# Front of a two-layer decoder step: the first two projections on rows without 1/rms, loads alternating by channel tile, step sizes from fp32 rows

## The chip, the cores and the metric

One Trainium2 chip; the kernel runs on one of its cores. The metric is the device time of one execution in microseconds, the median of the runs. The engines are PE (matrix multiply, with PEld, its weight loads), DVE (vector), ACT (scalar functions), POOL (a second, slower vector engine) and SP (here it only issues DMAs).

## The reference, cut to what matters

Two layers, an SSD layer and a pooling layer, on 1024 prompt tokens of one sequence and 64 sample tokens (8 sequences of 8). Everything is float32. The change touches the entry into the first layer:

```
rmsnorm(x, g) = x * rsqrt(mean(x*x) + EPS) * g
mod = silu(c) @ ada_w[i] + ada_b[i]; shift, scale, gate = split(mod, 3)
hn = rmsnorm(x, norm_g[i]) * (1 + scale) + shift
zxbcdt = hn @ w_in                    # z, xbc, dt_raw
conv = conv_b + sum(xp[:, k:k + L] * conv_w[k])   # 4 taps over time, on xbc; then silu
dt = softplus(dt_raw + dt_bias)       # step sizes, one per head
```

`shift` and `scale` are vectors over the channels, one for the prompt and one for each sample sequence. Behind this come the chunked scan, a gated norm, the output projection, and the pooling layer, which the change does not touch.

## The kernel before

All activations lie transposed: 128 channels on the partitions, 1088 tokens (1024 prompt, 64 sample) along the free axis, cut into three chunks `CH` of 364, 364 and 360. The model's 1024 channels are eight such tiles, k = 0 to 7. A float32 product is made of three matmuls in the faster format fp32r: the weights are split into `hi` and `lo` (L118 on ACT, L119 on DVE), the activations too, and hi·hi, hi·lo and lo·hi are summed in PSUM (`mm1`, L159 to L163).

`setup` (L173) issues in SP's queue all eight tiles of x, then the conditioning `ct`, the vectors `vec`, the constants `kc`; PE meanwhile runs 55 idle matmuls (`warm`). `front` (L1053) then squares each x tile on ACT (L1061, L1065), adds the squares up on DVE in `rst` (L1066), sums them over partitions with a matmul by ones (`ms_log`, L275) and makes 1/rms on ACT by Ln and Exp (L278, L290). For each channel tile `ada_first` loads two halves of the block of `ada_w` (L232), multiplies them with silu(c) (L236, tile `am`), copies the result (L241, `mp`), transposes it by two small matmuls (L245) and adds biases: `shf` and `scl` (L254, L255).

The projections come in groups of six tiles of 128 output channels (two B/C tiles, two x tiles, two z tiles), eight groups. Group 0 is special. Its first two tiles (PSUM `mm` and `p`, weights `w`) run with the channel tile k as outer loop, so that each normalised tile is used as soon as `modulate` (L292 to L313) has made it: on DVE t = x·scl·rst (L297), on ACT hi = t + shf (L303), on DVE lo (L304), and five short operations for the 64 sample columns, whose scl and shf differ by sequence (L309 to L313, one of them on ACT). The same loop makes the step sizes `pdt` in plain fp32, out of hi and lo in turn, four narrow matmuls each (L1104). Tiles 3 to 6 of the group (`proj_group`, weights `wh`, `wl`) then run on the stored hi and lo.

A finished tile is moved out of PSUM by ACT (`proj_chunk`, L353, L355) and convolved over time (`conv_tile`, L316): POOL makes the first tap (L322, and L323 for the sample columns), DVE adds three taps (L325, L326), ACT takes Tanh (L330) and DVE closes the product (L331). `dt_phase` turns `pdt` into step sizes in pieces.

The order on each engine is not that of the source: a scheduler that belongs to the language sets it when the program is built. Engines run their own row strictly in that order and wait for each other by semaphores. SBUF is handed out in 31 slots of one row of tokens (`Slots`); a tile that gets a slot waits for the last reader of what lay there.

## Time and profile before

| what | us |
|---|---|
| median of 3 runs (1702.71 to 1705.88) | 1704.2 |
| the profiled execution, its own time | 1702.18 |
| its span in the trace | 1700.4 |
| busy in the span: DVE, ACT, POOL | 1232.1, 732.9, 588.6 |
| first matmul of a projection | 23.50 |
| first matmul of tile 3 of group 0 | 74.96 |
| first matmul of tile 4 of group 0 | 87.03 |
| granted TensorE clock, mean | 0.994 of full |

Busy times overlap, engines run beside each other. In rows of the timeline the columns are start, duration, engine, line, operation, output<-inputs, shape, how many rows were merged, and in brackets the idle time ahead of it and what ended it. Each fp32 matmul leaves two records, each fp32r matmul one. The duration of an instruction overlaps the next one's somewhat, so a price is better read from one start to the next.

### The profile page before, as it was taken

Reading aid. Unit: us, or ns where it says so; the run is one execution under the profiler, and the core shown is the slowest. Engines: PE = TensorE matmul, PEld = TensorE weight load, DVE = VectorE, ACT = ScalarE, POOL = GpSimd, SP = SyncE. Lnnn points to the kernel's source line nnn. Section 1 sums busy time; section 2 is a strip of 40 time slices with the busy share of each in tenths; the row PEclk is TensorE's granted clock in tenths of the full one; section 3 lists DMA queues with packets and bytes.
Section 4 is the critical chain, followed back from the end, with each engine's and each line's share of the span. In section 5 each row is a group of like instructions: output and inputs, shape, how many; then the busy total and the mean of one; then the engine's idle time right before and its main releaser. Section 6 shows DMA issues by size and latency. Waiting matters only on the chain.

```text
span 1700.4 us, 29848 instructions
## 1 busy us (share of the span) xinstructions
PE 1664.1 (98%) x11701; PEld 1581.7 (93%) x11701; DVE 1232.1 (72%) x2144; ACT 732.9 (43%) x1498; POOL 588.6 (35%) x612
## 2 busy tenths in 40 slices
PE   8999999999999999999999998999999999999997
PEld 6899999999999999997889998999999999999996
DVE  5676767687676867687788448978889996555546
ACT  5344554655555555556542027533333333221123
POOL 0224435353444435262310024455666630000012
PEclk9999999999999999999999999999999999999999
DMA  9222243324334132415874132232323368511102
GB/s 357 78 69 86 91 148 90 125 85 145 98 103 149 50 129 74 155 48 181 298 248 171 38 122 72 73 120 102 112 98 109 108 219 323 189 50 50 38 26 105
DMA packets 104460, 209.72 MB, mean 123 GB/s; under 512 B 16224, under 2 KB 56320, under 8 KB 104320
## 3 DMA queue, kind: packets, MB, share of 16 engines
q1 hardware_dynamic: 104320, 207.82, 35.6%
q8 instruction: 92, 1.51, 0.4%
q14 instruction: 48, 0.39, 0.1%
HBM read 160.95 MB, written 46.84 MB: 122 GB/s over the span
## 4 chain that ended last, share of the span: by engine, by line
PE 81%; DVE 10%; DMA 3%; ACT 2%; issue 2%; POOL 1%; SPq 0%; DVEq 0%; ACTq 0%; POOLq 0%
PE mm L161 18%; PE mm L162 18%; PE mm L163 18%; PE st L905 4%; PE st L903 4%; PE st L904 4%; PE y L547 2%; PE S L556 2%; DVE ws L769 2%; PE y L551 1%; PE am L236 1%; PE tr L497 1%; PE tr L493 1%; DVE x L693 1%; PE pdt L1104 1%
## 5 line engine op out<-in xcount | busy, mean ns | idle before, releaser
L161 PE MATMUL mm<-hh,wh 128*128 128x364 f32 (+1 forms) x1104 | 366.0, 331 | 0.0
L163 PE MATMUL mm<-hh,wl 128*128 128x364 f32 (+1 forms) x1104 | 363.0, 329 | 0.0
L162 PE MATMUL mm<-hl,wh 128*128 128x364 f32 (+1 forms) x1104 | 363.0, 329 | 0.0
L161 PE MATMUL mm<-gh,wh 128*128 128x364 f32 (+3 forms) x768 | 252.9, 330 | 4.6 <-DVE gs L696 2.6
L163 PE MATMUL mm<-gh,wl 128*128 128x364 f32 (+3 forms) x768 | 252.9, 329 | 0.0
L162 PE MATMUL mm<-gl,wh 128*128 128x364 f32 (+3 forms) x768 | 252.3, 329 | 0.2 <-DVE gl L681 0.2
L118 ACT ACTIVATE wh<-wr 128x1024 fp32r<-128x1024 f32 (+1 forms) x97 | 95.7, 986 | 283.6 <-PE mm L162 259.1
L693 DVE SCALAR_TENSOR_TENSOR x<-mm,gat,x 128x364 f32<-128x364 f32 (+3 forms) x192 | 108.9, 571 | 147.3 <-PE mm L163 146.6
L161 PEld LDWEIGHTS mm<-hh,wh 128*128 128x128 f32 x1104 | 207.6, 188 | 4.5 <-issue 2.8
L162 PEld LDWEIGHTS mm<-hl,wh 128*128 128x128 f32 x1104 | 207.5, 188 | 1.3 <-issue 1.0
L163 PEld LDWEIGHTS mm<-hh,wl 128*128 128x128 f32 x1104 | 207.5, 188 | 0.8 <-issue 0.4
L325 DVE SCALAR_TENSOR_TENSOR xbc<-raw,cwh,xbc 128x1024 f32<-128x1024 f32 x96 | 137.9, 1437 | 34.7 <-POOL xbc L322 34.7
L161 PEld LDWEIGHTS mm<-gh,wh 128*128 128x128 f32 x768 | 144.4, 188 | 7.7 <-issue 3.6
L709 POOL TENSOR_TENSOR ss<-ss,sq 128x364 f32<-128x364 f32 (+1 forms) x24 | 25.6, 1069 | 352.9 <-ACT sq L708 352.9
L162 PEld LDWEIGHTS mm<-gl,wh 128*128 128x128 f32 x768 | 144.2, 188 | 1.1 <-issue 0.6
L163 PEld LDWEIGHTS mm<-gh,wl 128*128 128x128 f32 x768 | 144.4, 188 | 0.6 <-issue 0.5
L905 PE MATMUL st<-hh,w 128*128 128x272 f32 x448 | 129.2, 288 | 0.0
L903 PE MATMUL st<-hh,w 128*128 128x272 f32 x448 | 129.2, 288 | 0.0
L904 PE MATMUL st<-hl,w 128*128 128x272 f32 x448 | 128.9, 288 | 0.0
L532 POOL TENSOR_TENSOR ea<-xbc,ea 128x512 f32<-128x512 f32 x56 | 82.8, 1479 | 119.1 <-ACT ea L491 107.7
L119 DVE TENSOR_TENSOR wl<-wr,wh 128x1024 fp32r<-128x1024 f32 (+1 forms) x97 | 109.9, 1133 | 14.2 <-ACT wh L118 14.0
L322 POOL TENSOR_SCALAR xbc<-raw,cwh 128x1024 f32<-128x1024 f32 x32 | 53.2, 1662 | 149.7 <-ACT raw L353 103.6
(279 smaller groups left out, 3966.6 us busy)
## 6 DMA issues: line engine op xcount, KB each, us to landing
wr<-win SPq DMA_DIRECT2D x48, 512.0 KB, 4.2
acb<-acd SPq DMA_DIRECT2D x64, 256.0 KB, 3.8
wr<-pin SPq DMA_DIRECT2D x32, 512.0 KB, 3.5
x<-xT SPq DMA_DIRECT2D x16, 544.0 KB, 8.1
gyd<-xbc SPq DMA_DIRECT2D x16, 544.0 KB, 2.9
gr<-gyd SPq DMA_DIRECT2D x16, 544.0 KB, 6.9
pld<-pl SPq DMA_DIRECT2D x16, 544.0 KB, 2.8
zgd<-pz SPq DMA_DIRECT2D x16, 544.0 KB, 2.7
```

Of the source, the lines that this page charges most:

```text
L118: self.nc.scalar.activation(hi[:, :nk, :], raw[:, :nk, :], AF.Copy)
L119: self.nc.vector.tensor_tensor(out=lo[:, :nk, :], in0=raw[:, :nk, :], in1=hi[:, :nk, :].bitcast(F32), op=ALU.subtract)
L161: nc.tensor.matmul(ps[:, :n], hi[:, k, :], ah[:, a:a + n], start=first, stop=False)
L162: nc.tensor.matmul(ps[:, :n], hi[:, k, :], al[:, a:a + n], start=False, stop=False)
L163: nc.tensor.matmul(ps[:, :n], lo[:, k, :], ah[:, a:a + n], start=False, stop=last)
L322: nc.gpsimd.tensor_scalar(dst[:, :NP], raw[:, 0:NP], w[0], b, op0=ALU.mult, op1=ALU.add)
L325: nc.vector.scalar_tensor_tensor(out=dst[:, :NP], in0=raw[:, k:k + NP], scalar=w[k], in1=dst[:, :NP], op0=ALU.mult, op1=ALU.add)
L532: nc.gpsimd.tensor_tensor(out=ea, in0=C[:, tok].unsqueeze(1).to_broadcast([P, 4, 128]), in1=ea, op=ALU.mult)
L693: nc.vector.scalar_tensor_tensor(out=x[d][:, a:a + pn], in0=ps[:, :pn], scalar=self.gat[l][:, d, 8:9], in1=x[d][:, a:a + pn], op0=ALU.mult ...
L903: nc.tensor.matmul(ps[c][:, :QUART], hi[:, k], xh[:, t], start=(k == 0), stop=False)
L904: nc.tensor.matmul(ps[c][:, :QUART], hi[:, k], xl[:, t], start=False, stop=False)
L905: nc.tensor.matmul(ps[c][:, :QUART], lo[:, k], xh[:, t], start=False, stop=(k == 3))
```

## The change

- Only ct is loaded ahead of x; then x and the two ada halves of channel tile 0, vec, kc, the two weight tiles, and from there on x and the ada halves of one channel tile after another (`x_load`, `ada_load`). `warm` runs 30 matmuls instead of 55.
- `raw_split` makes u = x·scl without 1/rms, split into `uh` (ACT) and `ul` (DVE), and puts ten more columns behind the 64 sample ones: shf of the nine sequences and a zero. The first two projections run on u, so that their third chunk is 370 wide and also yields the projected shift. The last four slots are ten columns longer for that.
- 1/rms is needed when these two tiles leave PSUM: `raw_chunk` multiplies by `rst` on DVE and adds the projected shift on ACT (before: one ACT copy).
- The normalised rows (`modulate`) are now made after that, beside the third projection, which has the channel tile as outer loop; the fourth to sixth run as before.
- The step sizes come from the fp32 product x·scl·rst that `modulate` leaves in x (four narrow matmuls per channel tile instead of eight); the shift comes by 32 tiny matmuls `pds` and enters as a bias in `dt_phase`.
- A staging tile `st` in the scan of the samples shares the buffer of `xl`.

```
+    def raw_split(self, k):
+        nc, x, sc = self.nc, self.xs[k], self.scl[0]
+        hi, lo = self.slots.get("uh", F32R, full=True), self.slots.get("ul", F32R, full=True)
+        nc.scalar.activation(hi[:, :NP], x[:, :NP], AF.Copy, scale=sc[:, k, 8:9])
+        nc.vector.scalar_tensor_tensor(out=lo[:, :NP], in0=x[:, :NP], scalar=sc[:, k, 8:9], in1=hi[:, :NP].bitcast(F32), op0=ALU.mult, op1=ALU.subtract)
+        t = self.mt.tile([P, 416], F32, tag="mt", bufs=2, name=self.name("us"))
...
+        nc.scalar.activation(t[:, NS:NS + 9], self.shf[0][:, k, :], AF.Copy)
+        nc.gpsimd.memset(t[:, NS + 9:NS + 10], 0.0)
+        nc.scalar.activation(hi[:, NP:SLOT], t[:, :NS + 10], AF.Copy)
+        nc.vector.tensor_tensor(out=lo[:, NP:SLOT], in0=t[:, :NS + 10], in1=hi[:, NP:SLOT].bitcast(F32), op=ALU.subtract)
+        return hi, lo
+
+    def raw_chunk(self, G, ii, c, ps, rst, sh):
...
+        nc.vector.tensor_tensor(out=o, in0=ps[:, :pn], in1=rst[:, a:a + pn], op=ALU.mult)
+        nc.scalar.activation(o, o, AF.Identity, bias=sh[:, 8:9])
...
+            self.conv_tile(G["ti"][ii], raw, dst, G["ncv"][:, ii])
...
         for k in range(8):
+            if k < 7:
+                self.x_load()
+                self.adaw.append(self.ada_load(k + 1))
+                self.ada_first(k + 1)
+            u = self.raw_split(k)
+            for i in range(2):
+                for c, (a, n) in enumerate(CH):
+                    self.mm1(pst[i][c], ws[i], k, u, (a, n + (10 if c == 2 else 0)), k == 0, k == 7)
...
+        for i in range(2):
             self.proj_begin(G, i)
+            sh = self.gp.tile([P, 9], F32, tag=f"psh{i}", name=f"psh{i}")
+            nc.scalar.activation(sh, pst[i][2][:, 360:369], AF.Copy)
+            for c in range(3):
+                self.raw_chunk(G, i, c, pst[i][c], rst, sh)
...
         for k in range(8):
             hi, lo = sl.get("hh", F32R), sl.get("hl", F32R)
-            for a, n in CH if k == 0 else ((0, TOK),):
-                self.modulate(0, k, xs[k], rst, hi, lo, a, n, xs[k][:, a:a + n])
+            self.modulate(0, k, xs[k], rst, hi, lo, 0, TOK, xs[k])
+            self.hn.append((hi, lo))
+            for c in range(3):
+                self.mm1(ps[c], w, k, (hi, lo), CH[c], k == 0, k == 7)
+            for j in range(4):
+                o, n, tp = slice(32 * j, 32 * j + 32), 320 if j == 3 else 256, (0, 32 * j)
+                nc.tensor.matmul(pdt[o, :n], wdt[:, k, :], xs[k][:, 256 * j:256 * j + n], start=k == 0, stop=k == 7, tile_position=tp)
+                nc.tensor.matmul(pds[o, :9], wdt[:, k, :], self.shf[0][:, k, :], start=k == 0, stop=k == 7, tile_position=tp)
...
-            st = gp.tile([P, 256], F32R, tag="st", bufs=1, name=self.name("st"))
+            st = gp.tile([P, 256], F32R, tag="xl", bufs=1, name=self.name("st"))
```

What the scheduler makes of it, at three places. First PE, in the loop over the channel tiles (`am` is the ada block, `uh`/`ul` and `hh`/`hl` the activations, `w` the two weight tiles with their splits). Before, from the ada block of one tile into the next:

```order
L236 MATMUL am_528<-ada_524,scp 32x256 x4
L236 MATMUL am_528<-ada_526,scp 32x256 x4
L161 MATMUL mm_346<-hh_543,w_13_308 128x364
L162 MATMUL mm_346<-hl_544,w_13_308 128x364
L163 MATMUL mm_346<-hh_543,w_14_309 128x364
L245 MATMUL am_528<-kc,mp_537 128x9 x2
L161 MATMUL mm_347<-hh_543,w_13_308 128x364
```

Now:

```order
L241 MATMUL am_459<-ada_455,scp 32x256 x4
L164 MATMUL mm_241<-uh_474,w_4_212 128x364
L164 MATMUL mm_242<-uh_474,w_4_212 128x364
L164 MATMUL mm_243<-uh_474,w_4_212 128x370
L164 MATMUL p_244<-uh_474,w_6_218 128x364
L164 MATMUL p_245<-uh_474,w_6_218 128x364
L164 MATMUL p_246<-uh_474,w_6_218 128x370
L241 MATMUL am_459<-ada_456,scp 32x256 x4
L165 MATMUL mm_241<-ul_475,w_4_212 128x364
L166 MATMUL mm_241<-uh_474,w_5_213 128x364
L165 MATMUL mm_242<-ul_475,w_4_212 128x364
L250 MATMUL am_459<-kc,mp_468 128x9 x2
```

The two ada halves now stand apart, six matmuls on `uh` between them, and the pdt matmuls are gone from the loop.

Second DVE, where the normalised rows are made (`hl` is their lo part, `xbc_781`/`xbc_798` before and `xbc_673`/`xbc_700` now are the convolved tiles 1 and 2). Before, the end of the loop over the channel tiles and the first convolution:

```order
L297 SCALAR_TENSOR_TENSOR x_154<-x_154,scl_237,rst_247 128x1024
L310 TENSOR_TENSOR x_154<-x_154,scl_237 128x64
L434 MEMSET dtu_1046 128x128
L311 TENSOR_TENSOR x_154<-x_154,shf_235 128x64
L304 SCALAR_TENSOR_TENSOR hl_738<-x_154,shf_235,hh_737 128x1024
L313 TENSOR_TENSOR hl_738<-x_154,hh_737 128x64
L325 SCALAR_TENSOR_TENSOR xbc_781<-raw_340,cwh,xbc_781 128x1024
```

Now, the end of the second convolution and the first channel tile:

```order
L330 SCALAR_TENSOR_TENSOR xbc_700<-raw_686,cwh,xbc_700 128x1024
L331 SCALAR_TENSOR_TENSOR xbc_700<-raw_686,cwh,xbc_700 128x64
L330 SCALAR_TENSOR_TENSOR xbc_700<-raw_686,cwh,xbc_700 128x1024
L336 SCALAR_TENSOR_TENSOR xbc_673<-raw_659,xbc_673 128x1088
L331 SCALAR_TENSOR_TENSOR xbc_700<-raw_686,cwh,xbc_700 128x64
L330 SCALAR_TENSOR_TENSOR xbc_700<-raw_686,cwh,xbc_700 128x1024
L331 SCALAR_TENSOR_TENSOR xbc_700<-raw_686,cwh,xbc_700 128x64
L309 SCALAR_TENSOR_TENSOR hl_736<-x_142,shf_200,hh_735 128x1024
L314 TENSOR_TENSOR x_142<-x_142,rst_222 128x64
L336 SCALAR_TENSOR_TENSOR xbc_700<-raw_686,xbc_700 128x1088
L315 TENSOR_TENSOR x_142<-x_142,scl_202 128x64
L302 SCALAR_TENSOR_TENSOR x_247<-x_247,scl_202,rst_222 128x1024
```

Before, all eight `hl` stood ahead of the convolutions; now both convolutions stand ahead of the first `hl`, and seven more channel tiles follow them.

Third ACT at the same place (`hh` is the hi part; the Tanh has the convolved tile as its input). Before:

```order
L303 ACTIVATE hh_701<-x_152,shf_235 128x1024
L312 ACTIVATE hh_701<-x_152 128x64
L241 ACTIVATE mp_653<-am_644 128x256
L303 ACTIVATE hh_737<-x_154,shf_235 128x1024
L312 ACTIVATE hh_737<-x_154 128x64
L353 ACTIVATE raw_340<-mm_346 128x364
```

Now:

```order
L308 ACTIVATE hh_735<-x_142,shf_200 128x1024
L335 ACT_TABLE_LOAD
L335 ACTIVATE raw_659<-xbc_673 128x1088
L335 ACTIVATE raw_686<-xbc_700 128x1088
L308 ACTIVATE hh_762<-x_247,shf_200 128x1024
L317 ACTIVATE hh_735<-x_142 128x64
```

The Tanh of both convolved tiles now stand between `hh` of channel tile 0 and that of channel tile 1; before, they came behind all eight.

More of the change, by code (lines that the diff above doesn't have):

```diff
@@ L57, in add_wide, with get @@
         self.pools.update({t: (pool, WIDE) for t in self.b})
-    def get(self, name, dtype=F32, wide=False, short=False):
+    def get(self, name, dtype=F32, wide=False, short=False, full=False):
         older = short and self.a and self.b and self.freed.get(self.b[0], 0) <= self.freed.get(self.a[0], 0)
-        tag = (self.b if self.b and (wide or older or not self.a) else self.a).pop(0)
+        free = self.b if self.b and (wide or older or not self.a) else self.a
+        tag = free.pop(free.index(next(t for t in free if t in self.long)) if full else 0)
         pool, w = self.pools[tag]
@@ L214, in setup, with x_load, ada_load @@
             nc.gpsimd.memset(t, 0.0)
+    def x_load(self):
+        self.xs.append(self.slots.get("x"))
+        self.nc.sync.dma_start(self.xs[-1], self.io["xT"][len(self.xs) - 1])
+    def ada_load(self, kt):
+        raws = [self.slots.get("ada") for _ in range(2)]
+        for hh in range(2):
+            self.nc.sync.dma_start(raws[hh][:, :1024].rearrange("p (a b) -> p a b", a=4), self.io["adaA"][0, kt][:, 4 * hh:4 * hh + 4, :])
+        return raws
     def warm(self, n):
@@ L1114, in front @@
+        sl.free(rst, wdts)
+        dt = self.dt_phase(pdt, pds)
+        next(dt)
+        for c in range(3):
+            self.proj_chunk(G, 2, c, ps[c])
+        for i, _ in enumerate(self.proj_group(G, 3)):
+            if i > 2:
                 next(dt, None)
```

115 lines of the change are left out of this document (53 added, 62 removed).

## The prediction

> **What bounds the kernel now.** I read the page first, then the table by stretches of time, then the timeline of the first 130 us engine by engine.
>
> ```profile
> PE 1664.1 (98%) x11701; PEld 1581.7 (93%) x11701; DVE 1232.1 (72%) x2144; ACT 732.9 (43%) x1498; POOL 588.6 (35%) x612
> ```
>
> TensorE is the bound, so a change in the front is worth whatever it moves the point from which TensorE never waits again. The stretches show where that point is now (columns: stretch, its length, busy PE, PEld, DVE, ACT, POOL with counts, granted clock, DMA share, GB/s):
>
> ```profile
> 23.50:30.10 6.60, 6.25 (x27) 3.50 (x27) 4.58 (x9) 2.10 (x4) 1.95 (x2) 0.52 1.02 407
> ...
> 50.00:60.00 10.00, 10.00 (x91) 8.22 (x93) 8.49 (x20) 5.19 (x9) 0.00 (x0) 1.00 0.19 59
> ...
> 80.00:90.00 10.00, 10.00 (x62) 10.00 (x61) 9.16 (x13) 5.88 (x9) 4.09 (x9) 1.00 0.03 7
> 90.00:100.00 10.00, 10.00 (x62) 10.00 (x61) 9.79 (x17) 2.91 (x4) 2.99 (x5) 1.00 0.14 52
> ```
>
> From 40 us on PE is busy without a gap, but between 80 and 100 us DVE is at 92 and 98%: an engine with no room left. The marks against which I hold everything are starts on PE: the first projection matmul, the first of the third projection (weights `wh`), the first of the fourth.
>
> ```profile
> 23.50 1.18 PE L161 MATMUL mm<-hh,w 128*128 128x364 f32 x2 [1.85 <-ACT hh L303]
> ...
> 74.96 0.43 PE L161 MATMUL mm<-hh,wh 128*128 128x364 f32 x1
> ...
> 87.03 0.33 PE L161 MATMUL mm<-hh,wh 128*128 128x364 f32 x1
> ```
>
> So projections 1 and 2 take 23.50 to 74.96, the third 12.07 us. All later rows of normalised x lie ready by then, so the fourth projection's start is the mark: **before, 87.03 us.** Nothing later waits (10.00 of 10.00 in every stretch), so what that mark moves, the end moves.
>
> **Part 1: the earlier start.** Loads are paced by DMA:
>
> ```profile
> 5.92 1.11 ACT L1065 ACTIVATE sq<-x 128x1088 f32<-128x1088 f32 x1 [0.25 <-DMA x<-xT]
> 7.29 1.11 ACT L1065 ACTIVATE sq<-x 128x1088 f32<-128x1088 f32 x1 [0.26 <-DMA x<-xT]
> ...
> 14.16 1.30 ACT L1065 ACTIVATE sq<-x 128x364 f32<-128x364 f32 x3 [0.29 <-DMA x<-xT]
> 18.62 0.16 PEld L236 LDWEIGHTS am<-ada,scp 128*32 128x32 f32 x8 [0.75 <-DMA ada<-adaA]
> 19.90 0.16 PEld L236 LDWEIGHTS am<-ada,scp 128*32 128x32 f32 x8 [1.12 <-DMA ada<-adaA]
> 21.16 1.06 ACT L118 ACTIVATE w<-wr 128x1024 fp32r<-128x1024 f32 x1 [0.17 <-DMA wr<-win]
> ```
>
> An x tile lands every 1.37 us, a half of an ada block or a weight tile every 1.27, and ct, vec, kc and wdt together about 3.2 (14.16 to 18.62 less one ada half). The new queue before the first product holds ct, one x (first landing 4.6 before), two ada halves, vec, kc, one weight tile. With the small ones at 2.8: 4.6 + 0.8 + 2.5 + 2.0 + 1.3 = 11.2; then ACT splits the weights (1.06) and makes uh (1.15): first matmul at **13.5 us**, 10 us earlier (12.5 to 14.5). The second channel tile needs a second weight tile, scv, x and two ada halves more (11.2 + 1.3 + 0.4 + 1.4 + 2.5 = 16.8), then the last ada half's matmuls 0.6, mp 0.4, the p2 pair and scl 1.2, a short copy 0.2, uh 1.15 and the hand-overs, 4.2 in all (prices below): PE starts k=1 at **21.0**. The weights of projection 3 now stand behind the last ada half in SP's queue and land at 16.8 + 6 x 3.9 + 1.7 = 42, long before they are needed.
>
> **Part 2: the pace of the eight channel tiles.** What PE pays per tile, from the steady loop of before:
>
> ```profile
> 37.94 0.33 PE L163 MATMUL mm<-hh,w 128*128 128x364 f32 x1
> 38.20 0.64 PE L236 MATMUL am<-ada,scp 128*32 128x256 f32 x8
> 38.77 0.43 PE L162 MATMUL mm<-hl,w 128*128 128x360 f32 x1
> ...
> 39.70 0.33 PE L163 MATMUL p<-hh,w 128*128 128x364 f32 x1
> 39.87 0.33 PE L162 MATMUL p<-hl,w 128*128 128x360 f32 x1
> ...
> 50.05 0.33 PE L163 MATMUL mm<-hh,w 128*128 128x364 f32 x1
> 50.22 0.61 PE L245 MATMUL am<-kc,mp 128*128 128x9 f32 x4
> 50.69 0.41 PE L161 MATMUL mm<-hh,w 128*128 128x364 f32 x1
> ...
> 64.72 0.32 PE L163 MATMUL p<-hh,w 128*128 128x360 f32 x1
> 64.97 0.75 PE L1104 MATMUL pdt<-hh,wdt 128*32 128x256 f32 x8
> ...
> 66.18 0.44 PE L161 MATMUL mm<-hh,w 128*128 128x364 f32 x1
> ```
>
> Start to start, a matmul is 0.167; an ada half put between two costs 38.77 - 37.94 - 0.17 = 0.66, the p2 pair 0.47, the eight pdt matmuls of hi and lo 1.29. New, per tile: 18 matmuls 3.0 (ten more columns in every third are 10/364 of 0.167: nothing), two ada halves 1.32, p2 0.47, no pdt: 4.79. One wait is added. ACT squares x of the next tile but one (1.11) ahead of uh, so from the p2 pair:
>
> ```profile
> 49.78 0.38 ACT L241 ACTIVATE mp<-am 128x256 f32<-128x256 f32 x1 [0.73 <-PE am L236]
> ...
> 50.94 0.23 DVE L254 TENSOR_SCALAR shf<-am,vec 128x9 f32<-128x9 f32 x1 [0.55 <-PE am L245]
> 51.09 0.28 DVE L255 TENSOR_SCALAR scl<-am,adab,vec 128x9 f32<-128x9 f32 x1
> ...
> 53.02 1.14 ACT L303 ACTIVATE hh<-x,shf 128x1024 fp32r<-128x1024 f32 x1
> ```
>
> shf starts 0.72 after p2, a short copy 0.2, square 1.1, uh 1.15, hand-overs: 3.35; PE has p2, ten matmuls and one ada half in that time, 2.8. It waits 0.55: **5.35 per tile**. DMA needs 1.37 + 2.54 = 3.9, DVE 1.2 + 1.2 + four short ones, ACT some 3.1: all below. The stretch 23.50:30.10 shows a clock of 0.52 behind the wait for x; such a stretch costs half of 6.6 us, and I take 2 for it behind the gap at 18 to 21. k=2 starts at 21.0 + 4.8 + 0.2 + 2 = 28.0, k=7 at 28.0 + 5 x 5.35 = 54.8.
>
> ```profile
> 16.05 2.40 PE L275 MATMUL ms<-rst,ones 128*128 128x364 f32 x6 [0.16 <-DVE rst L1066]
> ...
> 17.88 0.56 ACT L278 ACTIVATE rst<-ms,eps 128x364 f32<-128x364 f32 x1 [0.25 <-PE ms L275]
> ...
> 19.72 0.50 ACT L290 ACTIVATE rst<-rst 128x360 f32<-128x360 f32 x1
> ```
>
> Its 18 matmuls and three sums (0.8 each) end at 60.1; Ln and Exp make the last third of 1/rms ready at **61.3** (55 to 64).
>
> **Part 3: what is late next.** DVE now has everything that needs 1/rms in one row, and the third projection eats its output as it is made. Prices:
>
> ```profile
> 57.22 1.28 DVE L297 SCALAR_TENSOR_TENSOR x<-x,scl,rst 128x1024 f32<-128x1024 f32 x1
> 58.42 0.22 DVE L310 TENSOR_TENSOR x<-x,scl 128x64 f32<-128x64 f32 x1
> 58.67 0.23 DVE L311 TENSOR_TENSOR x<-x,shf 128x64 f32<-128x64 f32 x1
> 58.81 1.22 DVE L119 TENSOR_TENSOR wl<-wr,wh 128x1024 fp32r<-128x1024 f32 x1
> ...
> 74.19 1.28 DVE L325 SCALAR_TENSOR_TENSOR xbc<-raw,cwh,xbc 128x1024 f32<-128x1024 f32 x1 [7.23 <-POOL xbc L322]
> ...
> 84.89 0.48 DVE L403 SCALAR_TENSOR_TENSOR dta<-dtv 128x320 f32<-128x320 f32 x1
> ```
>
> A wide operation moves DVE on by 1.20, a short one by 0.13 to 0.25 (0.18 taken); the two convolutions with one closing product ran 74.19 to 84.89, 10.7. In the built program the wide eviction products of tiles 1 and 2 come first, then x of channel 0, then **both convolutions, then hl of channel 0**, which the third matmul of the third projection needs. Also ACT's hh of channel 1 stands behind the two Tanh, which wait for the convolutions. From 61.3: the last four evictions 1.3; x of channel 0 1.2 (63.8); POOL's first product, which the convolution waits for, by
>
> ```profile
> 72.96 1.20 POOL L322 TENSOR_SCALAR xbc<-raw,cwh 128x1024 f32<-128x1024 f32 x1 [45.71 <-ACT raw L355]
> 74.14 1.44 POOL L323 TENSOR_SCALAR xbc<-raw,cwh 128x64 f32<-128x64 f32 x1
> ```
>
> is 2.6 to 3 behind the last eviction: 65.1. Convolutions and one short operation 10.9: 76.0. Then hl of channel 0, the second closing product and 14 wide operations of channels 1 to 7: 16 x 1.20 = 19.2, and 34 short ones 6.1: the last hl at **101.3**. PE has its last nine matmuls behind it: 1.5. Fourth projection at **102.8**, 15.8 us after 87.03. PE itself needs only 12.0 for the third projection and 8 x 0.65 for pdt from the fp32 rows (half the 1.29); the 32 tiny pds matmuls fall into its wait.
>
> Behind the mark DVE has 10.9 less to do than before, since the two convolutions lie ahead of it, so I expect no new wait there. Costed at nothing, with their cover: the shared buffer of `st` and `xl` (covered by the projection matmuls woven into the scans; two short ACT copies, 0.5 us, in each of 8 groups if not); 30 for 55 warm matmuls (they run before the first load has landed); the new dt path (DVE's short operations, counted among the 34).
>
> **The sum.** The profiled run took 1702.18 (span 1700.4), 2 us under the median of the three runs, 1704.2. 1702.18 + 15.8 = 1718.0; on the median **1720**. Bounds: 1/rms at 55 or 64 (-6, +3), short operations at 0.13 or 0.25 (-2, +2), convolutions uncontended at 9.5 or 12 (-1, +1): 1711 to 1726, and 1727 with the clock below.
>
> **Clock.** PE will wait about 11 us for hl of channel 0, and the row 23.50:30.10 says what follows a wait here: half clock for 6.6 us. Nine matmuls and pdt at 0.52 are 4.1 per channel against DVE's 2 x 1.20 + 4 x 0.18 = 3.1, so one such stretch adds about 1 us, which is in the upper bound. The Trainium skill, TensorE: Matmul & The Clock Gate, Part 1, says that an idle window of about 3.4 us halves TensorE's clock and about as long a busy one restores it. By that rule the cost would be half of 3.4 us per gap, 1.7 us, less than the 2 I take behind the gap at 18 to 21; the trace's 6.6 us decides.
>
> **Rivals.**
> 1. *DVE does not gate* (faster). With 1/rms at 61.3, PE could be through the third projection at 61.3 + 2.5 + 12.0 + 5.2 = 81.0, 6 us before 87.03: 1698. It decides at DVE needing less than 24 us from 1/rms to the last hl (87.0 - 61.3 - 1.5); I count 40. For it: the earlier start is real. Against: 24 wide operations alone are 28.8, and the order is fixed when the program is built. 0.08.
> 2. *Clock stays half through the third projection* (slower still). PE's 4.1 instead of DVE's 3.1 a channel tile over 8 tiles: +8, 1728. For it: the wait is longer than any in the front now. Against: before, it came back while PE was kept busy. 0.17.
> 3. *The tiles run at the pace of the loads*, 3.9 instead of 5.35, no clock loss: 1/rms 13 us earlier, 48, and the mark at 89.5: +2.5, 1706.7, no change to be told. It decides at PE needing under 3.9; it needs 4.79. 0.05.
> 4. The forecast: 0.70.
>
> **Chances.** A measurement tells 0.2% (3.4 us) from no change. Faster 0.08 (rival 1), same 0.05 (rival 3), slower 0.87 (forecast and rival 2). The range 1711 to 1730 takes in the forecast's bounds and rival 2, and leaves out 1 and 3, 0.13.
>
> **What would show it.** First projection matmul on PE near 13.5; its starts per channel tile 5.35 apart with short waits for uh; 1/rms near 61; PE's longest wait, some 10 us, ended by DVE's first hl; DVE without gap from there to about 101; fourth projection near 103, and all behind it shifted by that much. Wrong if PE's third projection takes about 15 us instead of 40, or if the stretch behind the front shows PE idle that before did not have.

## The result and the profile after

The changed kernel takes 1727.9 us (median of four, 1725.15 to 1729.01) against 1703.5 (four runs; the 1704.2 above was of three): ratio 1.0139, 95% interval 1.0123 to 1.0154. Forecast were 1720 and a range of 1711 to 1730. The profiled execution took 1725.15 us, its span 1723.4, against 1702.18 and 1700.4; the accounts below are made with these, 23.0 us apart.

TensorE's timeline of the changed kernel first (start, duration, instruction, idle time before it and who ended it): the first products of the first three channel tiles, the longest wait, and the mark of the prediction, the fourth projection's first product.

```profile
13.33 0.60 PE L164 MATMUL mm<-uh,w 128*128 128x364 f32 x2 [1.78 <-ACT uh L1064]
22.97 0.77 PE L164 MATMUL mm<-uh,w 128*128 128x364 f32 x3 [1.77 <-ACT uh L1064]
31.45 0.77 PE L164 MATMUL mm<-uh,w 128*128 128x364 f32 x3 [1.16 <-ACT uh L1064]
37.08 0.77 PE L164 MATMUL mm<-uh,w 128*128 128x364 f32 x3 [0.49 <-ACT uh L1064]
81.69 0.67 PE L165 MATMUL mm<-hl,wh 128*128 128x364 f32 x1 [9.96 <-DVE hl L309]
107.05 0.43 PE L164 MATMUL mm<-hh,wh 128*128 128x364 f32 x1 [0.26 <-ACT raw L358]
```

The first product comes 10.2 us earlier than before, as meant. The mark comes 20.0 us later: 107.05 against 87.03. In between, ScalarE's last third of 1/rms and VectorE's row behind it (first x, first convolution product, first and last wide low part):

```profile
64.74 0.49 ACT L295 ACTIVATE rst<-rst 128x360 f32<-128x360 f32 x1
```

```profile
66.42 1.28 DVE L302 SCALAR_TENSOR_TENSOR x<-x,scl,rst 128x1024 f32<-128x1024 f32 x1
69.32 1.28 DVE L330 SCALAR_TENSOR_TENSOR xbc<-raw,cwh,xbc 128x1024 f32<-128x1024 f32 x1 [1.62 <-POOL xbc L327]
80.35 1.28 DVE L309 SCALAR_TENSOR_TENSOR hl<-x,shf,hh 128x1024 fp32r<-128x1024 f32 x1
103.02 1.28 DVE L309 SCALAR_TENSOR_TENSOR hl<-x,shf,hh 128x1024 fp32r<-128x1024 f32 x1 [0.39 <-ACT hh L308]
```

1/rms is there at 65.23, the mark 41.8 us behind it, and VectorE works nearly all that time. The table by stretches (length, busy PE, PEld, DVE, ACT, POOL, granted clock, DMA share, GB/s) shows who had work:

```profile
10.00:20.00 10.00, 7.38 (x47) 5.27 (x38) 5.46 (x8) 4.79 (x7) 0.10 (x1) 0.83 1.03 409
20.00:30.00 10.00, 7.73 (x54) 5.25 (x50) 3.93 (x9) 4.13 (x8) 0.10 (x1) 0.83 1.02 408
...
70.00:80.00 10.00, 1.74 (x68) 1.25 (x64) 9.70 (x13) 2.40 (x2) 3.50 (x6) 0.50 0.00 0
80.00:90.00 10.00, 7.07 (x26) 4.91 (x26) 10.00 (x19) 3.85 (x6) 1.63 (x4) 0.53 0.03 7
90.00:100.00 10.00, 10.00 (x64) 6.21 (x63) 10.00 (x22) 5.39 (x8) 0.00 (x0) 1.00 0.00 0
```

TensorE is busy for 1.74 of 10 us at 70 to 80 while VectorE is at 9.70 to 10.00: there the front's bound is VectorE. From 84.5 on it is no longer VectorE alone. The last wait of TensorE that the timeline marks in the third projection is the one for x of the first channel, and from there to the projection's end its matmuls follow each other:

```profile
84.52 1.28 PE L1152 MATMUL pdt<-x,wdt 128*32 128x320 f32 x8 [1.25 <-DVE x L316]
...
98.56 0.76 PE L164 MATMUL mm<-hh,wh 128*128 128x364 f32 x3
...
104.55 0.77 PE L164 MATMUL mm<-hh,wh 128*128 128x364 f32 x3
```

Two channels take TensorE 5.99 (98.56 to 104.55) and VectorE 5.86 (its products of x at 90.53 and 96.39): the two engines are matched, and the chain of work that ended last, followed back from the end, leaves VectorE for TensorE at 84.5. The granted clock was low for TensorE at 10 to 30 and at 70 to 90.

Behind the mark the distance stays within 1 us of 20 for 1300 us, then TensorE loses 2.65 more. Its first product with `ph` (the hi part of the pooling layer's input), the stall behind that, and its last product, before and after:

```profile
1392.25 0.33 PE L161 MATMUL mm<-ph,wh 128*128 128x364 f32 x1
1394.73 0.43 PE L161 MATMUL mm<-ph,wh 128*128 128x364 f32 x1 [1.29 <-ACT ph L971]
...
1691.60 0.80 PE L277 MATMUL ms<-sq,ones 128*128 128x256 f32 x2
```

```profile
1412.17 0.33 PE L164 MATMUL mm<-ph,wh 128*128 128x364 f32 x1
1415.09 0.43 PE L164 MATMUL mm<-ph,wh 128*128 128x364 f32 x1 [1.75 <-ACT ph L978]
...
1418.09 0.50 PE L166 MATMUL mm<-ph,wl 128*128 128x364 f32 x1
1418.39 0.51 PE L164 MATMUL mm<-ph,wh 128*128 128x364 f32 x1
...
1714.17 1.22 PE L282 MATMUL ms<-sq,ones 128*128 128x256 f32 x2
```

From the first `ph` product to the last of all it is 299.35 us before and 302.00 after, where TensorE has the same matmuls in the same order. More than half of the 2.65 is clock: in the changed kernel the granted clock is 0.50 from 1417.17 to 1420.58 and products lie 0.30 apart, eleven of them, which costs some 1.5; in the kernel before it is 1.00 there and they lie 0.17 apart. The rest is longer waits, 0.4 for `ph` and 0.7 for weights (1.66 at 1436.59 against 0.92 at 1414.01). So the 23.0 are 20.0 in the front, 2.65 behind 1412, and 0.4 in small change.

### The profile page after: what moved, and what is told of

The parts are those of the page before. It is cut to its first block, busy times and chain, and to the rows that moved or that the text cites. A ratio compares the mean times of both kernels' runs of the same rounds, so it can differ in the third digit from the quotient of the medians.

```text
span 1723.4 us, 29802 instructions
## 1 busy us (share of the span) xinstructions
PE 1664.8 (97%) x11651; PEld 1574.7 (91%) x11651; DVE 1246.7 (72%) x2175; ACT 744.1 (43%) x1520; POOL 589.1 (34%) x620
## 4 chain that ended last, share of the span: by engine, by line
PE 83%; DVE 9%; DMA 3%; ACT 2%; issue 1%; POOL 1%; DVEq 0%; SPq 0%; ACTq 0%; POOLq 0%
PE mm L164 19%; PE mm L165 19%; PE mm L166 18%; PE st L912 4%; PE st L911 4%; PE st L910 4%; PE y L554 2%; PE S L563 2%; PE y L558 1%; DVE ws L776 1%; PE am L241 1%; PE tr L504 1%; PE tr L500 1%; DMA gr<-gyd 1%; DMA gin<-pld 1%
## 5 line engine op out<-in xcount | busy, mean ns | idle before, releaser
L700 DVE SCALAR_TENSOR_TENSOR x<-mm,gat,x 128x364 f32<-128x364 f32 (+3 forms) x192 | 108.9, 571 | 148.3 <-PE mm L166 147.7
L511 ACT ACTIVATE M<-acb,tkac 128x128 f32<-128x128 f32 x256 | 91.9, 393 | 26.4 <-PE y L554 25.4
```

What stands on the lines that cost most here:

```text
L511: nc.scalar.activation(M[:L, r, :L], acb[:L, r, :], AF.Relu, bias=tk["ac", cc][:L, col + r:col + r + 1], scale=-1.0)
L700: nc.vector.scalar_tensor_tensor(out=x[d][:, a:a + pn], in0=ps[:, :pn], scalar=self.gat[l][:, d, 8:9], in1=x[d][:, a:a + pn], op0=ALU.mult ...
```

## Experiments

Theory 1 is the forecast's: VectorE's row from 1/rms to the fourth projection sets the time. Its rival, theory 2, is the prediction's second rival: TensorE's halved clock behind the long wait. Theory 3 puts what came late ahead of 1/rms down to the clock in the first two waits, and theory 4, formed on e6, is that VectorE and GpSimd exclude each other.

All times are medians, beside 1703.4 to 1704.7 for the kernel before. "Mark" is the start of the fourth projection, "1/rms" the end of its last third (65.23 and 107.05 in the changed kernel, 41.8 apart). Marks come from one profiled execution of each kernel.

**e1: the convolutions of tiles 1 and 2 behind the third projection's rows.**

```diff
-            dst = self.slots.get("xbc")
-            self.conv_tile(G["ti"][ii], raw, dst, G["ncv"][:, ii])
-            G["out"].append(dst)
...
             sl.free(xs[k])
+        for i in range(2):
+            self.raw_conv(G, i)
+        self.proj_begin(G, 2)
```

> The changed kernel with the convolutions of tiles 1 and 2 written behind the third projection's modulate loop; nothing else differs. Theory 1 (VectorE's row between 1/rms and the fourth projection sets the end): the wait of 9.96 us for the first hl falls under 2 us and the last hl comes some 11 us earlier, at about 92. But tile 3 has no free raw buffer until the convolution of tile 1 has ended, about 6 us behind the last hl, so the fourth projection starts at 98 to 100 instead of 107.05, after a wait of about 6 us; 7 to 9 us less than 1727.9 if nothing else gets late, 1719 to 1721. If the step-size phase, which now stands behind four convolutions on VectorE, gets late in turn, part of that is lost again: up to 1725. Theory 2 (TensorE's halved clock behind the long wait is what costs): the wait is gone, so the clock stays at 1.0 and the third projection runs at TensorE's own pace, 2.65 us a channel, its last product by 91.

1723.5 us, ratio 1.0121 (1.0101 to 1.0142). VectorE's first low part, then TensorE's fourth projection and, later, the first product of the step-size phase (139.00 in the changed kernel):

```profile
69.36 1.28 DVE L309 SCALAR_TENSOR_TENSOR hl<-x,shf,hh 128x1024 fp32r<-128x1024 f32 x1
```

```profile
100.89 0.67 PE L164 MATMUL mm<-hh,wh 128*128 128x364 f32 x1 [5.30 <-ACT raw L358]
...
135.55 0.38 PE L448 MATMUL tr<-kc,dta 128*128 128x128 f32 x2
```

The wait of 10 us goes, and another of 5.30 takes its place: the raw buffer that the convolution holds. Behind that wait products lie 0.30 apart (half clock), and the 6.2 us won at the mark are 3.5 at the step-size phase. The two profiled executions differ by 2.0 only, and the interval overlaps that of the changed kernel, so the 4.4 between the medians is not sure. The third projection ended at 95.3 and not by 91: theory 2's 2.65 us a channel did not come. That does not decide between the theories, since TensorE's matmuls stand almost without a gap here too, 5.85 for two channels (83.42 to 89.27): the 2.65 was too low a price for TensorE's own row.

**e2: TensorE kept busy through the wait.** The products of ones have no use.

```diff
+                nc.tensor.matmul(ps[0][:, :364], w[0][:, 0, :], hi[:, :364], start=True, stop=False)
+                pw = self.pp.tile([P, 512], F32, tag="S", bufs=1, name="pw")
+                for _ in range(58):
+                    nc.tensor.matmul(pw[:, :128], self.ones, self.ones, start=True, stop=True)
```

> The changed kernel with 58 matmuls of ones by ones (no result used) put on TensorE around the first product of the third projection, 46 of them behind it, so that TensorE is busy through most of the wait for the first hl. Theory 1 (VectorE sets it): granted clock 1.0 instead of 0.53 at 80 to 90 us, but the fourth projection still starts at 106 to 107.5 and the time is 1726 to 1728.5. Theory 2 (the halved clock costs): nine matmuls and the step-size matmuls at full clock, the fourth projection 3 to 5 us earlier, 1723 to 1725.

1724.7 us, ratio 1.0119 (1.0101 to 1.0137); its interval overlaps that of the changed kernel. The stretch that had clock 0.53, and the mark:

```profile
80.00:90.00 10.00, 9.24 (x125) 7.31 (x124) 10.00 (x18) 3.82 (x5) 1.63 (x4) 1.00 0.02 5
```

```profile
106.78 0.43 PE L164 MATMUL mm<-hh,wh 128*128 128x364 f32 x1 [0.25 <-ACT raw L358]
```

With the clock at 1.00 the mark is 0.3 us earlier. The halved clock behind the long wait costs next to nothing: at full clock TensorE waits for VectorE again (0.53 for hl at 87.27). By the mark, theory 1. The median lies in theory 2's 1723 to 1725 and not in theory 1's range, but those 3 us do not come from the mark, and the two profiled executions (1725.71 and 1725.15) do not show them; they were not followed up.

**e3: the step-size product from fp32 rows alone, in the kernel before.**

```diff
-            for x in (hi, lo):
-                for j in range(4):
...
+            for j in range(4):
+                n = 320 if j == 3 else 256
+                nc.tensor.matmul(pdt[32 * j:32 * j + 32, :n], wdt[:, k, :], xs[k][:, 256 * j:256 * j + n], start=k == 0, stop=k == 7, tile_position=(0, 32 * j))
...
+        for k in range(8):
+            for j in range(4):
+                nc.tensor.matmul(pds[32 * j:32 * j + 32, :9], wdt[:, k, :], self.shf[0][:, k, :], start=k == 0, stop=k == 7, tile_position=(0, 32 * j))
```

> The kernel before with one part of the change alone: the step-size product from fp32 rows, four matmuls instead of eight per channel tile, and the shift's share in 32 small matmuls at the end. Theory 1: TensorE is the bound of the first two projections, so 8 x 0.65 us less some 1 us for the small ones is gained: the fourth projection at 82.5 to 83.5 instead of 87.03, 1699 to 1700 against 1703.5. Rival: VectorE, 92 and 98% busy at 80 to 100 us in the kernel before, takes over at once: TensorE waits there, under 1.5 us gained.

1698.7 us, ratio 0.9971 (0.9960 to 0.9982): this beats both kernels, and of the other runs only its variant e11 does. The fourth projection's first product:

```profile
82.22 0.33 PE L161 MATMUL mm<-hh,wh 128*128 128x364 f32 x1
```

4.8 us earlier than before, no new wait of TensorE up to 200 us: theory 1, and VectorE at 98% did not take over.

**e4: third and fourth projection both walked by channel tile, convolutions behind.**

```diff
-        w = self.stream_next()
-        ps = [self.mm_tile() for _ in range(3)]
+        w = [self.stream_next(), self.stream_next(False)]
+        ps = [[self.mm_tile() for _ in range(3)],
+              [self.pp.tile([P, 512], F32, tag=t, bufs=b, name=self.name("p1")) for t, b in (("y", 2), ("y", 2), ("S", 1))]]
...
+            for i in range(2):
+                for c in range(3):
+                    self.mm1(ps[i][c], w[i], k, (hi, lo), CH[c], k == 0, k == 7)
```

> The changed kernel with the third and the fourth projection both walked by channel tile (the fourth's sums in the banks that the second projection leaves), and the convolutions of tiles 1 and 2 behind that loop. Theory 1: TensorE then has 18 matmuls and four step-size matmuls, 3.65 us, for each channel that VectorE makes in 2.9 to 3.1, so it is the bound again: both projections end at about 69 + 8 x 3.65 = 98 to 100 instead of 107.05 + 12.05 = 119.1. Behind that it waits some 2 to 6 us for evictions, whose raw buffers the convolutions hold: 1710 to 1716 in all. Rival (all of VectorE's work up to the scan counts, in whatever order): the 20 us come back as waits of TensorE before 150 us, and the time is 1724 to 1728.

1718.5 us, ratio 1.0082 (1.0063 to 1.0101), 9.4 less than the changed kernel. The fifth projection's first product:

```profile
106.25 0.43 PE L164 MATMUL mm<-hh,wh 128*128 128x364 f32 x1 [0.61 <-ACT raw L358]
```

The fifth projection starts 12.8 us earlier than in the changed kernel (119.1), not 20: 1/rms was 1.8 later in this run (67.06), and TensorE took 3.97 for the last channel (101.67 to 105.64), not 3.65. A part comes back as a wait for VectorE (3.64 at 122.25), but not all: the rival is out. Theory 1 holds with a smaller gain than its 1710 to 1716.

**e5: TensorE kept busy in its first two waits for uh.** The loop stands in `ada_block` behind the p2 pair; the list holds 8 and 9.

```diff
+        for _ in range(self.fill.pop(0) if self.fill else 0):
+            nc.tensor.matmul(pm[:, 384:512], self.ones, mp[:, :128], start=True, stop=True)
```

> The changed kernel with TensorE kept busy in its first two waits for uh: 8 matmuls of no use behind the first channel tile's ada products, 9 behind the second's. Theory 3 (all that came later than forecast ahead of 1/rms is halved clock: products 0.30 us apart at 14.3 to 17.5 and at 24.8 to 28 us in the changed kernel): products 0.17 apart from the start, the second channel tile at 21.0 instead of 22.97, the third at 28.0 instead of 31.45, the last third of 1/rms at 61.7 instead of 65.2, and, since VectorE's row hangs on that, the fourth projection at 103.5 instead of 107.05; 1724.5 us. Rival (the ada loads set the second tile's start): it stays at 22.5 to 23, what TensorE gains it waits, and the time is within 1 us of 1727.9.

1720.7 us, ratio 1.0095 (1.0082 to 1.0108). Third channel tile and mark on TensorE, 1/rms on ScalarE:

```profile
28.57 0.60 PE L165 MATMUL mm<-uh,w 128*128 128x364 f32 x2
...
103.84 0.43 PE L165 MATMUL mm<-hh,wh 128*128 128x364 f32 x1 [0.26 <-ACT raw L361]
```

```profile
61.69 0.49 ACT L298 ACTIVATE rst<-rst 128x360 f32<-128x360 f32 x1
```

Products lie 0.17 apart from 16.6 us on, and 1/rms is 3.05 us earlier, the mark 3.2. The time fell by more than theory 3's 1724.5 asks for: the profiled executions differ by 6.05, of which 3.5 are there at the first `ph` product and 2.05 come behind it (299.95 against 302.00), where this run has no stretch at half clock. The second tile itself was late (24.34): the fillers write into the tile that also holds shift and scale, and VectorE read those only behind them. Theory 3 all the same. Its rival, that the loads set the start, is out: in e12 below, without that delay, TensorE takes the second tile's ada halves at 17.57 without a wait, and uh is ready at 21.5 (22.9 in the changed kernel), though the first product came 0.8 later there.

**e6: low parts of odd channels on GpSimd.** The branch taken for them is that of the second layer, where GpSimd makes lo.

```diff
-        if l:
+        if l or k % 2:
             nc.scalar.activation(t[:, :pn], t[:, :pn], AF.Identity, bias=sh)
             nc.scalar.activation(hi[:, a:a + pn], t[:, :pn], AF.Copy)
...
+                if k % 2 == 0:
+                    nc.tensor.matmul(pds[o, :9], wdt[:, k, :], self.shf[0][:, k, :], start=k == 0, stop=k == 6, tile_position=tp)
```

> The changed kernel with the low part of every second channel in the third projection made on GpSimd (ScalarE adds the shift to x first, so these channels leave the shift's step-size product), four wide operations off VectorE's row. Theory 1 (VectorE's row from 1/rms to the fourth projection): 4 x 1.20 less, the fourth projection at 102.3 to 103 instead of 107.05; the wait for the first hl stays 10 us; 1722.5 to 1724. Rival (GpSimd's or TensorE's own pace takes over): GpSimd needs 2.3 to 5 us for one (a third took 0.83 to 1.81 in a later stage), two channels of VectorE's row 4.7, and under 2 us are gained.

1734.2 us, ratio 1.0177 (1.0161 to 1.0193): 6.4 slower than the changed kernel, where both theories had it faster. In the profiled execution 1.8 stand ahead of 1/rms already (67.04), in a front that the edit does not touch. VectorE and GpSimd at one place:

```profile
100.16 1.27 DVE L302 SCALAR_TENSOR_TENSOR x<-x,scl,rst 128x1024 f32<-128x1024 f32 x1
101.36 2.38 DVE L318 TENSOR_TENSOR hl<-x,hh 128x64 fp32r<-128x64 f32 x1
103.67 0.21 DVE L316 TENSOR_TENSOR x<-x,shf 128x64 f32<-128x64 f32 x1
```

```profile
93.25 2.38 POOL L306 TENSOR_TENSOR hl<-x,hh 128x1024 fp32r<-128x1024 f32 x1 [1.54 <-ACT hh L305]
100.73 2.94 POOL L306 TENSOR_TENSOR hl<-x,hh 128x1024 fp32r<-128x1024 f32 x1 [5.10 <-ACT hh L305]
```

A short operation of VectorE, 0.21 us elsewhere, takes 2.38 and ends with GpSimd's; GpSimd's, 2.38 elsewhere, takes 2.94 when it begins while VectorE's is running. These do not run side by side. Each of the four low parts takes 1.20 off VectorE and holds it up for some 2.2: +4.0, and 1/rms to mark went from 41.8 to 45.7 (67.04 to 112.76). The Trainium skill, SBUF — State Buffer, section Who interferes with whom, says that VectorE and GpSimd share a pair of ports under an exclusive lock, and that an operation of VectorE with two SBUF inputs contends with one of GpSimd that reads SBUF. The rows agree: the short operation takes as long as GpSimd's does.

**e7: 4 fillers of e5's kind in the kernel of e3.**

```diff
+        self.fill = [4]
```

> The kernel before with the step-size product from fp32 rows, as in the run of that part alone, and 4 matmuls of no use in TensorE's wait of 1.85 us for the first hh, so that it idles some 1.0 us there. Theory 3: no halved stretch behind it (from 23.7 to 28.9 us products lay 0.30 apart in the run without the fillers); half of 5.2 us is gained, 1696 to 1697 against 1698.7. Rival: the halved clock has another cause than this wait, products stay 0.30 apart, 1698 to 1699.5.

1703.5 us, ratio 0.9992 (0.9982 to 1.0002). The first product came at 24.40, behind a wait of 1.85. The wait was as long as ever, for the same reason as in e5, and products stayed slow to 28.4. So the run tests nothing, and its time lies outside what either theory expected. Of the 2.5 us between the profiled executions of e7 and e3, 2.2 come behind the first `ph` product; the 4.8 between the medians stay open.

**e8: e4 with the fillers of e5.**

```diff
+        self.fill = [8, 9]
```

> The run with the third and fourth projection by channel tile and the convolutions behind, with the fillers of the first two waits as well. Theories 1 and 3 together: the last third of 1/rms 3.5 us earlier than without fillers, and TensorE, which bounds the two projections there, ends them 3.5 us earlier: 1714 to 1716 against 1718.5. Rival: the waits behind the two projections (for evictions and the step-size phase) take it back: 1717.5 to 1719.

1712.3 us, ratio 1.0045 (1.0030 to 1.0060), 6.2 less than e4; 1/rms at 63.63 against 67.06. The two gains add in the front: at the first `ph` product this run is 3.3 earlier than e4. Another 2.6 came behind it, where the matmuls are the same.

**e9: the changed kernel with the old step-size product** (no `pds`).

```diff
-                nc.tensor.matmul(pdt[o, :n], wdt[:, k, :], xs[k][:, 256 * j:256 * j + n], start=k == 0, stop=k == 7, tile_position=tp)
+            for x in (hi, lo):
+                for j in range(4):
...
+                    nc.tensor.matmul(pdt[32 * j:32 * j + 32, :n], wdt[:, k, :], x[:, 256 * j:256 * j + n].bitcast(F32),
```

> The changed kernel with the old step-size product: eight matmuls a channel tile from the high and low rows, instead of four from fp32 rows and the small ones of the shift. Theory 1 (TensorE has room in the third projection, since it waits for VectorE there): nine products and eight step-size matmuls are 1.5 + 1.29 = 2.8 us a channel against VectorE's 2.93, only the last channel's lie on the path: the fourth projection 0.5 to 1 later than 107.05, the time 1727.5 to 1729.5. Rival (the part is worth here what it is worth alone, 4.7 us): 1731.5 to 1733.

1736.5 us, ratio 1.0185 (1.0169 to 1.0202): 8.6 more, and the rival's 5 were too few. From 1/rms (67.12) to the mark it is 50.7 instead of 41.8. VectorE's last wide low part and TensorE's fourth projection:

```profile
104.89 1.28 DVE L309 SCALAR_TENSOR_TENSOR hl<-x,shf,hh 128x1024 fp32r<-128x1024 f32 x1 [0.41 <-ACT hh L308]
```

```profile
99.26 0.43 PE L164 MATMUL mm<-hh,wh 128*128 128x364 f32 x1
99.62 0.63 PE L1151 MATMUL pdt<-hh,wdt 128*32 128x256 f32 x6
100.18 0.43 PE L165 MATMUL mm<-hl,wh 128*128 128x364 f32 x1
...
117.80 0.43 PE L164 MATMUL mm<-hh,wh 128*128 128x364 f32 x1
```

TensorE ends 11.6 us behind VectorE's last: it is the bound here. Two channels take 7.9 (96.89 to 104.78), 3.95 each and not 2.8, because the built order breaks the step-size matmuls into groups between the products; at 99.26 a product that takes 0.17 moves TensorE on by 0.36 when a group follows. Theory 1's sum for TensorE was wrong. So TensorE had no room to spare in the third projection. With the short step-size product the two engines are matched there, as the rows from 98.56 on show; with the long one TensorE is the slower.

**e10: first convolution products of tiles 1 and 2 on ScalarE instead of GpSimd.**

```diff
-        nc.gpsimd.tensor_scalar(dst[:, :NP], raw[:, 0:NP], w[0], b, op0=ALU.mult, op1=ALU.add)
...
+        if act:
+            nc.scalar.activation(dst[:, :NP], raw[:, 0:NP], AF.Identity, bias=b, scale=w[0])
...
```

> The changed kernel with the first product of the convolutions of tiles 1 and 2 on ScalarE instead of GpSimd. Theory 4 (an operation of VectorE that begins beside one of GpSimd's waits for its end, and the other way round): VectorE's waits of 1.62 and 0.30 us and the 0.94 that its short product lost beside GpSimd's go: the first hl and the fourth projection 2 to 2.9 us earlier, 104.2 to 105 instead of 107.05, and the time 1725 to 1726. Rival (ScalarE's two products come as late as GpSimd's, or delay hh of the first channel): the fourth projection within 1 us of 107.05.

1724.7 us, ratio 1.0115 (1.0100 to 1.0129). 1/rms and mark:

```profile
66.72 0.49 ACT L295 ACTIVATE rst<-rst 128x360 f32<-128x360 f32 x1
```

```profile
105.87 0.44 PE L164 MATMUL mm<-hh,wh 128*128 128x364 f32 x1 [0.23 <-ACT raw L362]
```

The front ran 2.0 us later in this run (below), and the mark is 1.2 earlier all the same: 38.7 behind 1/rms instead of 41.8, 3.2 us off VectorE's row. Counted from 1/rms that is theory 4, a little above its 2 to 2.9; the mark itself misses the expected 104.2 to 105. What the run shows is the price of GpSimd's part: 1.92 of the 2.86 that theory 4 counts were waits for GpSimd's products, which a slow GpSimd explains as well, and 0.94 was time held up beside it. That the two exclude each other rests on the rows of e6.

**e11: 8 fillers in the kernel of e3, into columns of a bank that nobody reads.** The sums `pst` of the first two projections are laid out earlier for it.

```diff
+            nc.tensor.matmul(self.pst[1][2][:, 384:512], self.ones, mp[:, :128], start=True, stop=True)
```

> The kernel before with the step-size product from fp32 rows and 8 matmuls of no use in the wait for the first hh, written into columns of a bank that nobody reads, so that they hold nobody up (the 4 of the run before this wrote into the tile that holds the first channel's shift and scale, and VectorE read that only behind them: TensorE waited its 1.85 us all the same). Theory 3: the first product at 23.7, no halved stretch behind it, the fourth projection 2 to 2.6 us earlier than in the run of the step-size part alone: 1695.5 to 1697. Rival: the stretch stays halved, 1698 to 1699.5. Up to 2.5 us can go astray at some 300 us from the end, where the kernels of this study differ by that without a difference in their instructions; the fourth projection's start tells the theories apart all the same.

1700.0 us, ratio 0.9976 (0.9967 to 0.9986). First product and mark:

```profile
23.21 0.94 PE L162 MATMUL mm<-hh,w 128*128 128x364 f32 x2
...
80.04 0.33 PE L162 MATMUL mm<-hh,wh 128*128 128x364 f32 x1
```

No wait for the first hh, products 0.17 apart at once, and the mark 2.2 us before e3's, as theory 3 has it. The total does not show it: this run lost it again behind 1386.6, where it took 2.2 us more than e3 to the last product. So the time lies outside what either theory expected, and between e3 and e11 the medians tell nothing.

**e12: e8 with these fillers.**

```diff
-            nc.tensor.matmul(pm[:, 384:512], self.ones, mp[:, :128], start=True, stop=True)
+            nc.tensor.matmul(self.pst[1][2][:, 384:512], self.ones, mp[:, :128], start=True, stop=True)
```

> The run with the third and fourth projection by channel tile, the convolutions behind, and the fillers, which now write into columns of a bank that nobody reads. Theory 3: the first product again at 13.4 instead of 15.15 to 16.6, the second channel tile at 21.0 instead of 24.3 to 25.8, with products 0.17 apart: 1.5 to 2 us less than the 1712.3 with the fillers that held the scale up: 1710 to 1711. Rival (the pace of the later channel tiles, not the start, sets 1/rms): 1712 to 1713.

1710.9 us, ratio 1.0032 (1.0019 to 1.0045). The fifth projection (106.25 in e4):

```profile
100.56 0.43 PE L165 MATMUL mm<-hh,wh 128*128 128x364 f32 x1 [0.61 <-ACT raw L361]
```

1.4 less than e8, with intervals that overlap, and the third channel tile at 28.33 instead of 30.02 (31.45 in the changed kernel): theory 3, though the fillers themselves, which stand ahead of the first tile's last products, kept the second tile's first product at 22.88. With the clock of the front and the order of the stage behind it repaired, the raw front is still 0.32% behind the kernel before, and 12 us behind e3.

## Why the prediction was right, and where not

**The mechanism held up to 84.5 us; behind that, luck had a part.** The step that carried the forecast, 1/rms to mark through VectorE's row, was 41.5 us on paper (61.3 to 102.8) and 41.8 on the chip. Its first half is as forecast: x of the first channel at 66.42; convolutions and one short operation 11.0 (69.32 to 80.35) against 10.9; the wait for the first hl 9.96 against some 10. In the second half VectorE's last wide low part ended 39.1 behind 1/rms (104.30) against 40.0, but the mark came 2.75 behind that and not 1.5, because TensorE had its own row to finish. The forecast gave TensorE 12.0 for the third projection and 8 x 0.65 for the step sizes, 2.15 a channel; it took 3.0, as the built order breaks the step-size matmuls into groups: one alone between two products moves TensorE on by 0.66 (100.42 to 101.08), seven together by 1.20 (103.35 to 104.55). This price was the step that failed here. It did not show in the time, since 3.0 happens to be VectorE's pace too (2.93).

e10 took work out of VectorE's row, and the mark moved with it; e6 put work in, and it moved the other way; e9 put work into TensorE's, and it moved as well; e2 gave TensorE its clock back, and almost nothing moved. The built order, with both convolutions ahead of the first low part, is shown as the cause of the wait by e1. It is worth 6.2 us at the mark and not ten, and less at the end (2.0 between the profiled executions, 4.4 between the medians), since the convolutions' buffers and the step-size phase come next.

**The size was off ahead of 1/rms**, by 3.9 of the 4.2 us at the mark. The step that failed is the clock in part 2: I charged one half-clock stretch of 2 us, behind the wait at 18 to 21. There are two, at a granted clock of 0.50 from 14.29 to 17.70 and from 24.53 to 27.94. The first product came at 13.33, right, but behind a wait of 1.78, and the products behind it lay 0.30 apart to 17.5:

```profile
15.35 0.51 PE L165 MATMUL mm<-ul,w 128*128 128x364 f32 x1
15.66 0.50 PE L166 MATMUL mm<-uh,w 128*128 128x364 f32 x1
```

That put the second tile 2.0 late (22.97 for 21.0; e12 has its uh 1.4 earlier at full clock); from the second to the third tile it took 8.48 for 7.0, the 2 charged included (e12, at full clock, takes 5.45); and the pace took 0.9 (mostly 5.63 for 5.35, with a wait for uh of some 0.49 in most tiles as forecast at 0.55; e5 has the same 5.6, so it is not the clock). With the clock repaired, e5 has 1/rms at 62.2 and the mark at 103.84, within 1.1 us of the forecast. The way there is not the forecast's, though: its fillers held the second tile up to 24.34 for 21.0, and the third made most of that up (28.57 for 28.0) because the 2 us charged for the clock were not needed. Its 1720.7 also rests on a late stretch that took 299.95, nearly as before the change.

**Rival 2 has the right time for the wrong reason.** Its 1728 is what was measured, but e2 takes its condition away and leaves the mark where it was. The clock's loss was in the first two waits and in the late stretch, not in the third projection. The forecast's own bounds were 1711 to 1727, and 1727.9 lies just above them; it is inside the range because the range takes in rival 2. That is luck.

**The rest.** "All behind it shifted by that much" held to 1412 and failed by 2.65 there. The ground given for it, that nothing later waits, does not hold: the kernel before has TensorE wait for 3.50 us at 1040.05 and for 1.29 at 1394.73, among others. The stall at the first `ph` is followed by half clock after the change and not before; why the waits around it are longer was not found. The shared buffer of `st` and `xl` shows no cost: the offset is 20.0 at the mark and 19.9 at the first `ph`. The step-size part, costed at nothing inside the changed third projection, is worth 4.8 us alone (e3) and 8.6 in company (e9): without it, the front alone costs 32 to 33. Rivals 1 and 3 did not come: VectorE needed 39 us from 1/rms to the end of its last wide low part, not under 24, and the tiles ran 5.6 apart, not the loads' 3.9.

## What to carry to other kernels

An earlier start is worth only what the engine that finishes the stage does not have to do later: taking a factor (1/rms) out of the front and putting it back at eviction heaped evictions, convolutions and the rows of x onto one engine behind one event. Before moving work, add up that engine's row from the event to the point where TensorE no longer waits for it, price TensorE's own row as the built order has it, and look there for what stands ahead of the first result that TensorE needs. A change with two parts should be timed part by part: here one part alone gains 0.3%, and the other alone loses 1.9% (e9).

## What the runs showed of the hardware

**Operations of VectorE with two SBUF inputs and those of GpSimd exclude each other.** Beside e6, the changed kernel has it in its convolutions:

```profile
70.53 1.22 DVE L331 SCALAR_TENSOR_TENSOR xbc<-raw,cwh,xbc 128x64 f32<-128x64 f32 x1
...
72.86 0.28 DVE L331 SCALAR_TENSOR_TENSOR xbc<-raw,cwh,xbc 128x64 f32<-128x64 f32 x1
```

```profile
69.40 2.27 POOL L327 TENSOR_SCALAR xbc<-raw,cwh 128x1024 f32<-128x1024 f32 x1
```

The same short product takes 0.28 alone and 1.22 beside GpSimd, both counted as busy: "busy 10.00" of VectorE is not 10.00 of work. In e6's stretch 90 to 100 it has 15 instructions, in the changed kernel 22. A product with one input in PSUM is not held up: `x<-mm,gat,x` (L700) takes 0.60 at 884.90 with GpSimd at work since 884.41, as it does elsewhere.

**Short waits were followed by half clock, and the same code can lose more or less by it.** Waits of 1.78 and 1.77 us were enough. The Trainium skill, TensorE: Matmul & The Clock Gate, Part 1, gives an idle window of about 3.4 us. The trace has stretches at 0.50 of 3.41 us or twice that here, but ahead of the first one TensorE was not idle for 3.41 us; it was busy for 1.23 of them:

```profile
10.88:14.29 3.41, 1.23 (x7) 0.83 (x7) 2.59 (x5) 3.11 (x5) 0.00 (x0) 1.00 1.04 399
```

So no unbroken wait of that length is needed. How busy TensorE has to be, these records do not say: 1.48 of 3.41 kept the clock at 62.08 to 65.49 in the changed kernel, and 1.88 lost it at 18.85 to 22.26 in e3.

The same section says that the window runs freely, so that the cold stretch differs from run to run. The trace agrees: with one and the same front the third channel tile began at 31.45 in the changed kernel, 31.56 in e2, 33.27 in e4 and 33.48 in e10. Up to 0.9 of the 2.0 is there at the first product (13.33 to 14.21), ahead of any half clock; the rest is the second stretch at 0.50, from 24.53 to 27.94 in the changed kernel and from 22.50 to 29.33 in e4. So one profiled execution placed this front to no better than 2 us.

**A late stretch that differs by 4 us with the same matmuls.** From the first `ph` product to the last of TensorE the 14 kernels took 299.35 to 303.4 us, with the same matmuls in the same order. Part of it goes with the clock: the two without half clock behind the first `ph` took 299.35 and 299.95, the four with 6.83 us of it (e1, e7, e10, e11) 302.3 to 303.4, and those with 3.41 us 299.9 to 302.5. With a scatter of this size the total of one kernel can't tell apart edits of under 2 us in the front; marks in the trace can, counted from 1/rms where the front itself scatters.
